# First mixer: TensorE in a written order, a head's core within the next head's projection, and key products in 32-column blocks

## The chip, the cores and the metric

The kernel runs on one core of a Trainium2 chip. The metric is device time in microseconds of one execution, the median over several runs. The engines are TensorE (PE, with its weight loads shown as PEld), VectorE (DVE), ScalarE (ACT), GpSimd (POOL) and SyncE (SP, which only issues transfers here).

## The reference

Two transformer blocks work on 256 latent and 256 context tokens of width 1024. The first block has a gated linear attention in both directions (the first mixer), the second a latent softmax attention; each is followed by a mixture of 32 experts. Only the first mixer is touched:

```python
def gla_chunkwise(q, k, v, log_f, s0):          # chunks of 32 tokens, 8 heads of 128
    def step(s, blk):
        qc, kc, vc, gc = blk
        b = jnp.cumsum(gc, axis=-2)
        b_end = b[:, :, -1:, :]
        q_dec = qc * jnp.exp(b)
        scores = jnp.einsum('bhtc,bhsc->bhts', q_dec, kc * jnp.exp(-b))
        scores = jnp.where(lower_tri, scores, 0.0)
        o = jnp.einsum('bhts,bhsv->bhtv', scores, vc) + jnp.einsum('bhtc,bhcv->bhtv', q_dec, s)
        s_new = jnp.exp(b_end[:, :, 0, :])[..., None] * s + jnp.einsum('bhsc,bhsv->bhcv', kc * jnp.exp(b_end - b), vc)
        return s_new, o
    ...

def hgrn2_mixer(h_lat, h_ctx, w_in, lower_bound, out_norm_g, w_out, with_ctx_out):
    # p = h @ w_in gives q, z_fw, z_bw, v, g; f = lb + (1 - lb) sigmoid(z); k = 1 - f
    # forward and backward passes over context and latent tokens, summed
    # y = (rms_norm(o) * silu(g)) @ w_out
    ...
```

## The kernel before

All 512 tokens stand along the free dimension, in four tiles of 128. The first mixer works through eight heads. For a head, `L507` asks for its 2 MB of weights, and four projections (`q` = forward gate, backward gate, query, output gate) are made: each is 8 contraction steps of three products (`L513` to `L515`: high part by high part, high by low, low by high), 96 products of 128x512 in all. `split` (`L262` on ACT, `L264` on DVE) makes the high and low parts of 1024 weight columns, with three buffers. The values of four heads come from a value projection of the same size (`vstep`, `L283` to `L285`), once at the start and once before head 4; it holds all four accumulators named `mm`.

`dir_pre` makes, for each direction, decayed queries `eq`, keys `ek`, keys decayed to a tile's end `ke`, and `kx`, the keys of one half of a tile decayed to the middle, for products with the other half. `core(h)` then does, for the forward direction and after it for the backward one:

- queries `qm` (`L438`, DVE) and `qt` (`L440`, `L442`);
- scores into one PSUM bank per direction (`scP`): for each tile four products with 32 columns of keys, each at its own column position of the array (`L450`), and one with a block of 64 columns (`L454`). A product of float32 operands appears in the trace as two passes;
- masking into SBUF (`L456`, DVE), and the sum over both directions (`L460`);
- turned keys (`L465`), copied by ACT (`L467`), state products (`L471`), and the running state on ACT and DVE (`L473`, `L475`). The turned keys and the state products use the single PSUM bank `p4`, one after the other.

Then come the outputs (`L487`, bank `p5`), their norm (`L492` to `L494`), and the turned output (`L498`, bank `p4`), multiplied by the gate (`L499`).

Conditioning for later stages rides along: `ada_piece` multiplies one block of `ada_w` (1 MB, `L208`) with the conditioning vector, four products at four column positions (`L212`); eight pieces make a third, which ends with a DVE sum (`L218`, for one third also `L222`) and its turned sums (`L225`). Four pieces follow each of the first six heads' projections.

The order of instructions on each engine is set by the framework's scheduler: among the instructions that are ready by its own model of time, it takes the one that stands first in the program. `tc.manual_schedule(engines=...)`, used elsewhere in the kernel, keeps the program's order on the named engines instead. So before the change, TensorE's list interleaves `core(h)` with the projection of head h + 1 as the scheduler finds them ready.

Of the kernel before, what the change touches and what calls it, by code (L numbers as in the profile page):

```python
# [9 lines left out]
F32 = mybir.dt.float32  # L10
# [6 lines left out]
ALU = mybir.AluOpType  # L17
# [65 lines left out]
class K:  # L83
# [183 lines left out]
    def hgrn(self):  # L267
        tc, nc, I = self.tc, self.nc, self.I
        PE, V, S, G = nc.tensor, nc.vector, nc.scalar, nc.gpsimd
        with ExitStack() as left, ExitStack() as st:  # L270
# [8 lines left out]
            def vstep(acc, k, H, L):  # L279
                c = slice(k % 2 * 512, k % 2 * 512 + 512)  # L280
                for tt in range(4):
                    ts = slice(tt * 128, tt * 128 + 128)
                    PE.matmul(acc[tt], hH[:, k, ts], H[:, c], start=(k == 0), stop=False)  # L283
                    PE.matmul(acc[tt], hH[:, k, ts], L[:, c], start=False, stop=False)
                    PE.matmul(acc[tt], hL[:, k, ts], H[:, c], start=False, stop=(k == 7))  # L285

            with tc.tile_pool(name="hin", bufs=1, side="right", reuse_waits="tile") as ip:
                ss = self.sp.tile([128, 4], F32, tag="ss", name="ss")
# [35 lines left out]
                for k in range(8):  # L324
                    if k % 2 == 0:
                        H, L = self.split(raw[:, k * 512:k * 512 + 1024], wp, [128, 1024])
                    vstep(acc, k, H, L)
            self.dump("hT", hH)
            cw = st.enter_context(tc.tile_pool(name="hgb", bufs=1, side="right", reuse_waits="tile"))

# [44 lines left out]
                    self.ada_piece(*ada_todo.pop(0), self.mm, aring.tile([128, 2048], F32, tag="aw", name="aw", bufs=2),  # L375
                                   lambda: [hp.tile([128, 512], F32, tag="adx", name=f"ad{t}", bufs=4) for t in "bsg"])

            def vproj(i, V4):

                acc_ = acc  # L380
                if i:
                    acc_, raw = [self.mm() for _ in range(4)], self.slot()
                    nc.sync.dma_start(raw, I["hg_wv"][i])
                    for q in range(4):
                        H, L = self.split(raw[:, q * 1024:(q + 1) * 1024], wp, [128, 1024])
                        for k in (2 * q, 2 * q + 1):
                            vstep(acc_, k, H, L)
                for tt in range(4):
                    S.copy(V4[:, tt, :], acc_[tt])

            v4 = lambda t: t.rearrange("p (t c j) -> p t c j", t=4, c=2)

            def dir_pre(h, d, z):
# [26 lines left out]
                V.tensor_tensor(ek, s, ek, op=ALU.mult)  # L420
                ex = lambda i: e[:, :, i:4:2].rearrange("p t (c o) -> p t c o", o=1)
                sq_, sk_ = (ex(0), ex(1)) if d == 0 else (ex(1), ex(0))
                ke = cw.tile([128, 512], F32, tag="ke", name="ke", bufs=2)
                V.tensor_tensor(v4(ke), v4(ek), sk_.to_broadcast([128, 4, 2, 64]), op=ALU.mult)
                first = v4(ke)[:, :, d, :]
                kx = cw.tile([128, 4, 64], F32, tag="kx", name="kx", bufs=2)
# [1 line left out]
                V.tensor_tensor(first, first, e[:, :, 5 - d:6 - d].to_broadcast([128, 4, 64]), op=ALU.mult)  # L428
                return dict(eq=eq, ek=ek, ke=ke, kx=kx, sq=sq_, E=e)

            def core(h, V4, hh, dd, sq, gs, dst):
                vs = slice(hh * 128, hh * 128 + 128)
                Sst, qts, scs = [], [], []
                both = cw.tile([128, 512], F32, tag="on", name="both")
                for d in range(2):
                    x = dd[d]
                    qm = x["eq"]
                    V.tensor_tensor(qm, sq, x["eq"], op=ALU.mult)  # L438
                    qt = cw.tile([128, 512], F32, tag="qt", name="qt", bufs=2)
                    V.tensor_tensor(v4(qt), v4(qm), x["sq"].to_broadcast([128, 4, 2, 64]), op=ALU.mult)  # L440
                    second = v4(qt)[:, :, 1 - d, :]
                    V.tensor_tensor(second, second, x["E"][:, :, 4 + d:5 + d].to_broadcast([128, 4, 64]), op=ALU.mult)  # L442
                    qts.append(qt)
                    psc = scP[d]
                    for tt in range(4):
                        a = tt * 128
                        for c in range(4):
                            s0, c0 = a + c * 32, a + (c // 2) * 64
                            t0, n = (c0, 64) if c % 2 == d else (s0, 32)
                            PE.matmul(psc[c * 32:c * 32 + 32, t0:t0 + n], x["ek"][:, s0:s0 + 32], qm[:, t0:t0 + n],  # L450
                                      start=True, stop=True, tile_position=(0, c * 32))

                        t0 = a + 64 * (1 - d)
                        PE.matmul(psc[d * 64:d * 64 + 64, t0:t0 + 64], x["kx"][:, tt, :], qm[:, t0:t0 + 64], start=True, stop=True)  # L454
                    sc = scT[d]
                    V.copy_predicated(sc.rearrange("p (t j) -> p t j", t=4), masks[d].to_broadcast([128, 4, 128]),  # L456
                                      psc.rearrange("p (t j) -> p t j", t=4))
                    scs.append(sc)
                    if d:
                        V.tensor_tensor(both, scs[0], sc, op=ALU.add)  # L460
                    order = [0, 1, 2, 3] if d == 0 else [1, 0, 3, 2]
                    pk = self.sm()
                    for i in range(3):
                        tt = order[i]
                        PE.transpose(pk[:, i * 128:(i + 1) * 128], x["ke"][:, tt * 128:(tt + 1) * 128], self.ident)  # L465
                    kT = cw.tile([128, 384], F32, tag="kT", name="kT", bufs=1)
                    S.copy(kT, pk[:, 0:384])  # L467
                    pd = self.sm()
                    for i in range(3):
                        cs = slice(i * 128, i * 128 + 128)  # L470
                        PE.matmul(pd[:, cs], kT[:, cs], V4[:, order[i], vs], start=True, stop=True)  # L471
                    ss = cw.tile([128, 3, 128], F32, tag="S", name="S", bufs=2)
                    S.copy(ss[:, 0, :], pd[:, 0:128])  # L473
                    for i in range(1, 3):
                        V.scalar_tensor_tensor(ss[:, i, :], ss[:, i - 1, :], x["E"][:, order[i], 6:7], pd[:, i * 128:(i + 1) * 128],  # L475
                                               op0=ALU.mult, op1=ALU.add)
                    Sst.append((ss, {order[i + 1]: i for i in range(3)}))
                po = self.ac()
                for tt in range(4):
                    ts = slice(tt * 128, tt * 128 + 128)  # L480
                    ops = [(both[:, ts], V4[:, tt, vs])]
                    for d in range(2):
                        ss, pos = Sst[d]
                        if tt in pos:
                            ops.append((qts[d][:, ts], ss[:, pos[tt], :]))
                    for i, (l_, r_) in enumerate(ops):
                        PE.matmul(po[:, ts], l_, r_, start=(i == 0), stop=(i == len(ops) - 1))  # L487
                ssq = cw.tile([128, 4], F32, tag="ssq", name="ssq", bufs=2)
                on = cw.tile([128, 4, 128], F32, tag="on", name="on", bufs=1)
                for tt in range(4):  # L490
                    ts = slice(tt * 128, tt * 128 + 128)
                    S.activation(on[:, tt, :], po[:, ts], AF.Square, accum_out=ssq[:, tt:tt + 1])  # L492
                ssq = self.rstd(ssq, 128, 4, "rs4")
                V.tensor_tensor(on, po.rearrange("p (t j) -> p t j", t=4),  # L494
                                ssq.rearrange("p (t o) -> p t o", o=1).to_broadcast([128, 4, 128]), op=ALU.mult)
                pt = self.sm()
                for tt in range(4):
                    PE.transpose(pt[:, tt * 128:(tt + 1) * 128], on[:, tt, :], self.ident)  # L498
                V.scalar_tensor_tensor(dst(), pt, self.cols[:, 64:65], gs, op0=ALU.mult, op1=ALU.mult)  # L499

            for h in range(8):
                if h % 4 == 0:
                    V4 = cw.tile([128, 4, 512], F32, tag="V4", name="V4", bufs=2)
                    vproj(h // 4, V4)
                dd = []
                raw = self.slot()
                nc.sync.dma_start(raw, I["hg_w"][h])  # L507
                for q in range(4):
                    H, L = self.split(raw[:, q * 1024:(q + 1) * 1024], wp, [128, 1024])
                    p = self.mm()  # L510
                    for k in range(8):
                        c = slice(k * 128, k * 128 + 128)
                        PE.matmul(p, H[:, c], hH[:, k, :], start=(k == 0), stop=False)  # L513
                        PE.matmul(p, H[:, c], hL[:, k, :], start=False, stop=False)  # L514
                        PE.matmul(p, L[:, c], hH[:, k, :], start=False, stop=(k == 7))  # L515
                    if q < 2:
                        dd.append(dir_pre(h, q, p))
                    else:
                        t = cw.tile([128, 512], F32, tag=f"sq{q}", name=f"sq{q}", bufs=2)
                        self.sigmoid(t, p, -1)  # L520
                        V.tensor_tensor(t, t, p, op=ALU.mult)
                        if q == 2:
                            sq = t
                        else:
                            gs = t
                if h < 6:
                    ada_some(4)
                o7 = []

                def dst():  # L530
                    if h < 7:
                        return oT[:, h, :]
                    o7.append(cw.tile([128, 512], F32, tag="on", name="o7"))
                    return o7[0]
                if h == 5:
                    self.load_router(hp, 0)
                if h == 7:
                    self.router(hp, 0, self.mm())
                core(h, V4, h % 4, dd, sq, gs, dst)


            wop = [self.slot() for _ in range(2)]
# [990 lines left out]
```

## Time and profile before

| | us |
|---|---|
| median of 3 runs (1575.3 to 1577.18) | 1576.33 |
| the profiled execution | 1578.04 |
| its span, first to last instruction | 1576.3 |
| TensorE busy in the span | 1499.6 |
| DVE busy in the span | 813.2 |
| ACT busy in the span | 449.1 |
| stage of the eight heads' projections | 53 to 344 |

A line of the timeline reads: start, duration, engine, line and operation, what is written and read, shapes and count, and in brackets the engine's idle time before it and what ended that. Matmuls overlap, since their ends are modelled: what a matmul costs the engine is read from the start of the next one.

### The profile page before, as it was taken

How to read it: one execution, taken by the hardware profiler on the slowest of the kernel's cores; microseconds unless marked ns; L12 is line 12 of the kernel's file. 1: busy time of each engine (PE TensorE's matmuls, PEld its weight loads, DVE VectorE, ACT ScalarE, POOL GpSimd, SP SyncE). 2: the span in 40 equal slices, each digit the busy share in tenths (PEclk: the TensorE clock that was granted, in tenths of full speed). 3: DMA queues.
4: the chain of work that ended last, by engine and by line, in shares of the span. 5: the costliest groups of instructions: out<-in, count | busy, mean ns of one | idle time of the engine just before them, and what ended most of it. 6: DMA issues, size and time to landing. Idle time of an engine off the chain costs nothing. (4 is left out here: it accounts for less than half of the span.)

```text
span 1576.3 us, 20139 instructions
## 1 busy us (share of the span) xinstructions
PE 1499.6 (95%) x8009; PEld 825.2 (52%) x8010; DVE 813.2 (52%) x1675; ACT 449.1 (28%) x938; POOL 74.9 (5%) x101
## 2 busy tenths in 40 slices
PE   7999999999899999999999999989799999998997
PEld 4777787778644544544544454447444443433433
DVE  5776647775824544544544567674534332332333
ACT  4554445553411111111111145554411111111110
POOL 0000000001300000000000011310100000000000
PEclk9999999999799999999999999999899999999999
DMA  9454534414769999999999957344799999999997
GB/s 384 165 201 177 196 136 161 188 54 161 276 240 399 429 428 426 428 427 426 427 429 423 356 218 305 141 187 142 272 392 428 427 427 428 428 427 428 427 425 268
DMA packets 63127, 500.80 MB, mean 318 GB/s; under 512 B 7024, under 2 KB 16624, under 8 KB 32816
## 3 DMA queue, kind: packets, MB, share of 16 engines
q1 hardware_dynamic: 59296, 490.87, 76.5%
q10 hardware_dynamic: 2816, 7.26, 1.4%
q0 software_dynamic: 912, 1.27, 0.3%
q8 instruction: 67, 1.10, 0.3%
q14 instruction: 36, 0.29, 0.0%
HBM read 498.26 MB, written 1.11 MB: 317 GB/s over the span
## 5 line engine op out<-in xcount | busy, mean ns | idle before, releaser
L1038 PE MATMUL mm<-w,xT 128*64 128x512 f32 x2048 | 469.9, 595 | 19.8 <-DMA w<-in_wg_dram 16.4
L1038 PEld LDWEIGHTS mm<-w,xT 128*64 128x64 f32 x2048 | 146.8, 137 | 310.7 <-issue 266.3
L1089 DVE TENSOR_TENSOR tmp<-p,rG 128x512 f32<-128x512 f32 (+1 forms) x106 | 68.0, 644 | 132.7 <-PE p L1087 132.6
L1090 DVE TENSOR_TENSOR x<-x,tmp 128x512 f32<-128x512 f32 (+1 forms) x195 | 132.4, 679 | 6.7
L1089 DVE TENSOR_TENSOR tmp<-p,x 128x512 f32<-128x512 f32 (+1 forms) x68 | 44.4, 655 | 165.1 <-PE p L1087 165.1
L1069 PE MATMUL mm<-w,x 128*64 128x512 f32 (+1 forms) x544 | 116.3, 570 | 1.6 <-ACT x L1057 1.4
L1069 PE MATMUL mm<-w,hT 128*64 128x512 f32 (+1 forms) x544 | 113.9, 570 | 1.4 <-ACT hT L1057 1.4
L889 PE MATMUL p<-sel,h2H 128*128 128x256 f32 x384 | 101.8, 300 | 1.8 <-DVE sel L879 1.8
L513 PE MATMUL mm<-hH,wH 128*128 128x512 f32 x256 | 101.9, 398 | 0.3 <-ACT wH L262 0.3
L515 PE MATMUL mm<-hH,wL 128*128 128x512 f32 x256 | 101.3, 396 | 0.5 <-DVE wL L264 0.5
L514 PE MATMUL mm<-hL,wH 128*128 128x512 f32 x256 | 100.6, 393 | 0.0
L890 PE MATMUL p<-sel,h2L 128*128 128x256 f32 x384 | 98.5, 290 | 0.0
L1076 DVE SCALAR_TENSOR_TENSOR yL<-mm,wsl,yH 128x512 fp32r<-128x512 f32 (+1 forms) x68 | 48.7, 716 | 71.6 <-ACT yH L1075 71.6
L1075 ACT ACTIVATE yH<-mm,wsl 128x512 fp32r<-128x512 f32 (+1 forms) x68 | 45.1, 663 | 123.3 <-PE mm L1069 93.2
L889 PEld LDWEIGHTS p<-sel,h2H 128*128 128x128 f32 x384 | 76.7, 200 | 5.1 <-issue 2.4
L264 DVE TENSOR_TENSOR wL<-w,wH 128x1024 fp32r<-128x1024 f32 x55 | 67.0, 1221 | 23.5 <-ACT wH L262 22.0
L1086 PE MATMUL p<-yH,G 128*128 128x512 f32 (+1 forms) x174 | 76.2, 441 | 0.9 <-DVE tmp L1089 0.9
L890 PEld LDWEIGHTS p<-sel,h2L 128*128 128x128 f32 x384 | 76.3, 199 | 1.4 <-issue 0.8
L1069 PEld LDWEIGHTS mm<-w,x 128*64 128x64 f32 x544 | 45.6, 137 | 60.0 <-issue 45.6
L262 ACT CAST wH<-w 128x1024 fp32r<-128x1024 f32 x55 | 57.3, 1047 | 63.3 <-PE mm L514 32.8
L1069 PEld LDWEIGHTS mm<-w,hT 128*64 128x64 f32 x544 | 37.5, 137 | 65.8 <-issue 59.7
L1086 PEld LDWEIGHTS p<-yH,G 128*128 128x128 f32 x174 | 32.5, 187 | 65.8 <-issue 51.5
(392 smaller groups left out, 2119.2 us busy)
## 6 DMA issues: line engine op xcount, KB each, us to landing
w<-in_wg_dram SPq DMA_DIRECT2D x52, 2048.0 KB, 18.1
w<-in_wu_dram SPq DMA_DIRECT2D x52, 2048.0 KB, 21.4
w<-in_wd_dram SPq DMA_DIRECT2D x52, 2048.0 KB, 20.2
aw<-in_ada_w_dram SPq DMA_DIRECT2D x32, 1024.0 KB, 6.0
w<-in_wd_dram SPq DMA_DIRECT2D x48, 512.0 KB, 8.7
w<-in_hg_w_dram SPq DMA_DIRECT2D x8, 2048.0 KB, 7.9
w<-in_wg_dram SPq DMA_DIRECT2D x32, 512.0 KB, 7.8
w<-in_wu_dram SPq DMA_DIRECT2D x32, 512.0 KB, 9.5
```

What stands on the lines that cost most here:

```text
L262: nc.scalar.copy(H, raw)
L264: nc.vector.tensor_tensor(L, raw, H, op=ALU.subtract)
L513: PE.matmul(p, H[:, c], hH[:, k, :], start=(k == 0), stop=False)
L514: PE.matmul(p, H[:, c], hL[:, k, :], start=False, stop=False)
L515: PE.matmul(p, L[:, c], hH[:, k, :], start=False, stop=(k == 7))
L889: self.nc.tensor.matmul(o, self.h2H[:, tt, c], r, start=(tt == 0 and k == 0), stop=False)
L890: self.nc.tensor.matmul(o, self.h2L[:, tt, c], r, start=False, stop=(last and k == 1))
L1038: PE.matmul(p[a * 64:(a + 1) * 64, :], xT[:, k, a * 64:(a + 1) * 64], ws[a][:, k * 512:(k + 1) * 512], start=(k == 0), stop=(k == 7))
L1069: PE.matmul(p[a * 64:(a + 1) * 64, :], hT[:, j, a * 64:(a + 1) * 64], ws[a][:, j * 1024 + n * w_:j * 1024 + n * w_ + w_], start=(j == 0), ...
L1086: PE.matmul(pc, g, yH, start=True, stop=False)
L1089: V.tensor_tensor(t, pc, rG[vec(tt)][:, ns], op=ALU.mult)
L1090: adder.tensor_tensor(x[:, tt, ns], x[:, tt, ns], t, op=ALU.add)
```

## The change

The loop over heads becomes generators. `project(h)` makes the four projections in 32 steps of three products, `vproj` the second half of the values in 32 steps; `core(h)` gives way seven times. `beside` runs a projection and, after fixed steps of it, the next part of the previous head's core; the conditioning pieces come two by two after steps 7 and 24. Inside this block TensorE keeps the program's order; the other engines are scheduled as before. The scores of both directions are made in one go, after both directions' `qm`. The products with `kx`, 64 columns at a time for one direction, become 32-column products: for each tile, the two halves of both directions' blocks take the four column positions. `ke` has three buffers. The last head's core runs after the block, as before.

```diff
-                ke = cw.tile([128, 512], F32, tag="ke", name="ke", bufs=2)
+                ke = cw.tile([128, 512], F32, tag="ke", name="ke", bufs=3)
...
+            def scores(dd, qms):
+                for tt in range(4):
+                    a = tt * 128
+                    for d in range(2):
+                        for c in range(4):
+                            s0, c0 = a + c * 32, a + (c // 2) * 64
+                            t0, n = (c0, 64) if c % 2 == d else (s0, 32)
+                            PE.matmul(scP[d][c * 32:c * 32 + 32, t0:t0 + n], dd[d]["ek"][:, s0:s0 + 32], qms[d][:, t0:t0 + n],
+                                      start=True, stop=True, tile_position=(0, c * 32))
+                    for c in range(4):
+                        d = c // 2
+                        t0 = a + 64 * (1 - d)
+                        PE.matmul(scP[d][c * 32:c * 32 + 32, t0:t0 + 64], dd[d]["kx"][:, tt, c % 2 * 32:c % 2 * 32 + 32],
+                                  qms[d][:, t0:t0 + 64], start=True, stop=True, tile_position=(0, c * 32))
...
-                        t0 = a + 64 * (1 - d)
-                        PE.matmul(psc[d * 64:d * 64 + 64, t0:t0 + 64], x["kx"][:, tt, :], qm[:, t0:t0 + 64], start=True, stop=True)
...
+            def beside(job, side, ada=False):
+                next(side, None)
+                for i, _ in enumerate(job, 1):
+                    if ada and i in (7, 24):
+                        ada_some(2)
+                    if i in (7, 10, 12, 14, 16, 19, 25):
+                        next(side, None)
+
+            V4, side = values(acc), iter(())
+            with tc.manual_schedule(engines={mybir.EngineType.PE}):
+                for h in range(8):
+                    if h == 4:
+                        res = []
+                        beside(vproj(res), side)
+                        V4, side = res[0], iter(())
+                    res = []
+                    beside(project(h, res), side, h < 6)
+                    side = core(h, V4, *res, dst_of(h))
+                    if h == 5:
+                        self.load_router(hp, 0)
+            self.router(hp, 0, self.mm())
+            for _ in side:
+                pass
```

In the new `core`, the places where it gives way stand: after both `qm` (before the projection starts); after scores, `qt`, masks and their sum; after the forward direction's turned keys; after its state products; after the same two of the backward direction; and after outputs and norm.

More of the change, by code (lines that the diff above doesn't have):

```diff
@@ L285, in vstep @@
                     PE.matmul(acc[tt], hL[:, k, ts], H[:, c], start=False, stop=(k == 7))
+                    yield
             with tc.tile_pool(name="hin", bufs=1, side="right", reuse_waits="tile") as ip:
@@ L326, in hgrn @@
                         H, L = self.split(raw[:, k * 512:k * 512 + 1024], wp, [128, 1024])
-                    vstep(acc, k, H, L)
+                    for _ in vstep(acc, k, H, L):
+                        pass
             self.dump("hT", hH)
@@ L376, in ada_some, with values, vproj @@
                                    lambda: [hp.tile([128, 512], F32, tag="adx", name=f"ad{t}", bufs=4) for t in "bsg"])
[L378 to L387, printed above, removed]
+            def values(acc_):
+                V4 = cw.tile([128, 4, 512], F32, tag="V4", name="V4", bufs=2)
                 for tt in range(4):
                     S.copy(V4[:, tt, :], acc_[tt])
+                return V4
+            def vproj(res):
+                acc_, raw = [self.mm() for _ in range(4)], self.slot()
+                nc.sync.dma_start(raw, I["hg_wv"][1])
+                for q in range(4):
+                    H, L = self.split(raw[:, q * 1024:(q + 1) * 1024], wp, [128, 1024])
+                    for k in (2 * q, 2 * q + 1):
+                        yield from vstep(acc_, k, H, L)
+                res.append(values(acc_))
             v4 = lambda t: t.rearrange("p (t c j) -> p t c j", t=4, c=2)
@@ L429, in dir_pre, with core @@
                 return dict(eq=eq, ek=ek, ke=ke, kx=kx, sq=sq_, E=e)
-            def core(h, V4, hh, dd, sq, gs, dst):
-                vs = slice(hh * 128, hh * 128 + 128)
-                Sst, qts, scs = [], [], []
+            def scores(dd, qms):
[12 more added lines that the diff above has]
+                                  qms[d][:, t0:t0 + 64], start=True, stop=True, tile_position=(0, c * 32))
+            def core(h, V4, dd, sq, gs, dst):
+                vs = slice(h % 4 * 128, h % 4 * 128 + 128)
+                orders = [[0, 1, 2, 3], [1, 0, 3, 2]]
+                Sst, qts, qms = [], [], []
+                for d in range(2):
+                    qm = dd[d]["eq"]
+                    V.tensor_tensor(qm, sq, qm, op=ALU.mult)
+                    qms.append(qm)
+                yield
+                scores(dd, qms)
                 both = cw.tile([128, 512], F32, tag="on", name="both")
@@ L436, in core @@
                     x = dd[d]
-                    qm = x["eq"]
-                    V.tensor_tensor(qm, sq, x["eq"], op=ALU.mult)
                     qt = cw.tile([128, 512], F32, tag="qt", name="qt", bufs=2)
-                    V.tensor_tensor(v4(qt), v4(qm), x["sq"].to_broadcast([128, 4, 2, 64]), op=ALU.mult)
+                    V.tensor_tensor(v4(qt), v4(qms[d]), x["sq"].to_broadcast([128, 4, 2, 64]), op=ALU.mult)
                     second = v4(qt)[:, :, 1 - d, :]
@@ L443, in core @@
                     qts.append(qt)
[L444 to L451, printed above, removed]
-                        t0 = a + 64 * (1 - d)
[L454 to L461, printed above, removed]
+                for d in range(2):
+                    V.copy_predicated(scT[d].rearrange("p (t j) -> p t j", t=4), masks[d].to_broadcast([128, 4, 128]),
+                                      scP[d].rearrange("p (t j) -> p t j", t=4))
+                V.tensor_tensor(both, scT[0], scT[1], op=ALU.add)
+                for d in range(2):
+                    x, order = dd[d], orders[d]
+                    yield
                     pk = self.sm()
@@ L467, in core @@
                     S.copy(kT, pk[:, 0:384])
+                    yield
                     pd = self.sm()
@@ L477, in core @@
                     Sst.append((ss, {order[i + 1]: i for i in range(3)}))
+                yield
                 po = self.ac()
@@ L495, in core @@
                                 ssq.rearrange("p (t o) -> p t o", o=1).to_broadcast([128, 4, 128]), op=ALU.mult)
+                yield
                 pt = self.sm()
@@ L499, in core, with project @@
                 V.scalar_tensor_tensor(dst(), pt, self.cols[:, 64:65], gs, op0=ALU.mult, op1=ALU.mult)
[L501 to L504, printed above, removed]
+            def project(h, res):
                 dd = []
@@ L515, in hgrn @@
                         PE.matmul(p, L[:, c], hH[:, k, :], start=False, stop=(k == 7))
+                        if k < 7:
+                            yield
                     if q < 2:
@@ L521, in hgrn, with dst_of @@
                         V.tensor_tensor(t, t, p, op=ALU.mult)
[L522 to L528, printed above, removed]
+                        res.append(t)
+                    if q == 3:
+                        res.insert(0, dd)
+                    yield
+            o7 = []
+            def dst_of(h):
                 def dst():
@@ L534, in dst @@
                     return o7[0]
[L535 to L539, printed above, removed]
+                return dst
+            def beside(job, side, ada=False):
[19 more added lines that the diff above has]
+            for _ in side:
+                pass
             wop = [self.slot() for _ in range(2)]
```

## The prediction

> **What bounds the kernel now.** I began with the page's busy shares, then took the table by stages, then the timeline of the first mixer.
>
> ```profile
> PE 1499.6 (95%) x8009; PEld 825.2 (52%) x8010; DVE 813.2 (52%) x1675; ACT 449.1 (28%) x938; POOL 74.9 (5%) x101
> ```
>
> ```profile
> 53.00:344.00 291.00, 288.89 (x1920) 216.19 (x1921) 202.76 (x374) 151.47 (x301) 5.77 (x22) 1.00 0.42 159
> 344.00:357.00 13.00, 12.11 (x121) 8.90 (x120) 9.67 (x20) 7.37 (x14) 4.15 (x4) 0.74 0.01 2
> 433.00:870.00 437.00, 433.43 (x2177) 205.24 (x2178) 202.35 (x356) 49.89 (x91) 0.00 (x0) 1.00 0.98 408
> ```
>
> The columns are the stretch, its length, busy time of PE, PEld, DVE, ACT and POOL, granted clock, DMA share and GB/s. The eight heads fill 53 to 344. There PE is idle for 2.1 of 291 us at full clock, and DMA is used for 0.42. So this stage costs what TensorE spends on it, and a microsecond less of TensorE's own time is a microsecond gained, as long as no new idle time takes its place. From 433 to 870 the expert weights keep DMA at 0.98; that stretch starts when the mixer is done and slides with it. Busy time says nothing of whether TensorE is well used, since ends are modelled and overlap, so I read starts:
>
> ```profile
> 75.92 0.64 PE L212 MATMUL mm<-aw,cS 128*32 128x512 f32 x4
> ...
> 111.38 1.92 PE L212 MATMUL mm<-aw,cS 128*32 128x512 f32 x16
> 113.12 0.29 PE L450 MATMUL p<-eq,ek 128*32 128x64 f32 x8
> 113.34 0.33 PE L454 MATMUL p<-eq,kx 128*64 128x64 f32 x2
> 113.59 0.31 PE L450 MATMUL p<-eq,ek 128*32 128x64 f32 x8
> ...
> 116.87 0.33 PE L454 MATMUL p<-eq,kx 128*64 128x64 f32 x2
> 117.13 0.50 PE L513 MATMUL mm<-hH,wH 128*128 128x512 f32 x1
> 117.46 0.40 PE L514 MATMUL mm<-hL,wH 128*128 128x512 f32 x1
> ...
> 343.23 0.39 PE L513 MATMUL mm<-hH,wH 128*128 128x512 f32 x1
> 344.14 0.39 PE L514 MATMUL mm<-hL,wH 128*128 128x512 f32 x1
> 344.68 0.49 PE L610 MATMUL mm<-rw,colBf 128*2 128x36 f32 x10
> ```
>
> A head's period is 111.38 - 75.92 = 35.46 us. A projection product starts every (344.14 - 343.23)/4 = 0.227. The first one after other work takes 117.46 - 117.13 = 0.33, and the last one before a narrow-column product 344.68 - 344.14 - 0.227 = 0.31, so a return and an entry into column mode cost about 0.1 and 0.09. The scores of a head take 117.13 - 113.12 = 4.01 us: eight rounds of 0.22 for eight 32-column passes and 0.25 to 0.26 for two passes of the 64-column block.
>
> **The scores.** Removed: per 128 tokens, two 64-column blocks (four passes). Added: four 32-column products (eight passes). A head has 96 passes after and 80 before, all in one column mode, four columns side by side.
>
> ```profile
> L450 PE MATMUL p<-eq,ek 128*32 128x64 f32 x224 | 17.4, 230 | 0.8 <-DVE eq L438 0.7
> L450 PE MATMUL p<-eq,ek 128*32 128x32 f32 x224 | 14.6, 206 | 0.0
> ```
>
> The round at 113.59 spans 0.31 from first start to last end; less one instruction's mean of 0.22 its eight starts lie within 0.09. A 512-column pass of four costs (113.12 - 111.38)/4 = 0.435, which is 0.85 ns a column, so 64 columns stream in 0.054. Where no mode change follows, the next round can start 0.09 + 0.054 = 0.145 after the first. Twelve rounds give 1.75 us a head. The lower bound is streaming alone: each column strip gets 64 + 32 + 64 columns twice, 320 x 0.85 ns = 0.27 for 128 tokens, 1.1 us a head. The upper bound keeps a round at the 0.25 of the block round: 3.0 us. I take 1.75, since it rests on the same instruction.
>
> The Trainium skill (TensorEngine Tiling, Key Properties) says that changing the tiling mode drains TensorE; the two extra 0.1s above agree. Against the change speaks the skill's TensorE: Matmul & The Clock Gate (Part 1), by which starts never come closer than about 25 ns: 96 passes would be an estimated 2.4 us a head, 5 us worse over eight heads than my sum. The starts within 0.09 for eight passes are closer than that, so the row decides here.
>
> **The written order.** Each projection has 32 steps of three products (0.68 us); the previous head's core comes after steps 7 (scores), 10 (turned keys), 12 (state products), 14 and 16 (the same for the second direction), 19 (outputs) and 25 (turned output), two conditioning pieces each after steps 7 and 24. The other blocks cost:
>
> ```profile
> 201.37 0.49 PE L465 MATMUL p<-ident,ke 128*128 128x128 f32 x3
> 201.90 0.48 ACT L467 COPY kT<-p 128x384 f32<-128x384 f32 x1 [2.01 <-PE p L465]
> 202.43 0.94 PE L471 MATMUL p<-V,kT 128*128 128x128 f32 x6
> 203.12 0.48 PE L284 MATMUL mm<-wL,hH 128*128 128x512 f32 x1
> 203.40 0.27 ACT L473 COPY S<-p 128x128 f32<-128x128 f32 x1 [1.02 <-PE p L471]
> 203.70 0.73 DVE L475 SCALAR_TENSOR_TENSOR S<-S,e,p 128x128 f32<-128x128 f32 x2 [1.98 <-ACT S L473]
> 204.58 0.52 PE L465 MATMUL p<-ident,ke 128*128 128x128 f32 x3
> 204.86 0.47 PE L284 MATMUL mm<-wL,hH 128*128 128x512 f32 x1
> ...
> 207.32 0.49 PE L487 MATMUL p<-S,qt 128*128 128x128 f32 x2
> 209.35 0.48 PE L285 MATMUL mm<-wH,hL 128*128 128x512 f32 x1
> ...
> 212.03 0.69 DVE L494 TENSOR_TENSOR on<-p,rsr 128x512 f32<-128x512 f32 x1
> 212.87 0.63 PE L498 MATMUL p<-ident,on 128*128 128x128 f32 x4
> 213.25 0.48 PE L284 MATMUL mm<-wL,hH 128*128 128x512 f32 x1
> ```
>
> A head without waits: 96 x 0.227 = 21.8; eight returns and two column entries 1.0; two conditioning blocks of 16 at 1.74, 3.5; turned keys 2 x 0.28; state products 2 x 0.69; outputs 2.03 for 18 passes, so 2.25 for 20; turned output 0.38; scores 1.75. That is 32.6, against 35.46: 2.8 us. Seven heads give 19.8, of which scores are 15.8. The eighth head runs after the projections: its scores save 2.3. There the 344 to 357 row shows a granted clock of 0.74, and
>
> ```profile
> 350.83 0.68 DVE L438 TENSOR_TENSOR eq<-sq,eq 128x512 f32<-128x512 f32 x1
> ```
>
> makes the second direction's queries, behind the first direction's DVE work; the change makes both ahead of the scores. I take 2 us for that (0 to 5). Gross gain: 24.
>
> Now the waits. TensorE no longer goes round a late operand, so what is behind it waits too, all projection products above all.
> - Turned keys, step 10 to 12: the copy at 201.90 follows, state products start 1.06 after the keys. Written distance 0.28 + 1.45 = 1.7. Nothing.
> - State products to the second direction's turned keys, which need the same single PSUM bank: 204.58 - 202.43 = 2.15 when ACT and DVE are free. Written distance 0.69 + 1.45 = 2.14. No slack, so whatever sits ahead in ACT or DVE's queue is paid. The late case is
>
> ```profile
> 128.03 0.94 PE L471 MATMUL p<-V,kT 128*128 128x128 f32 x6
> ...
> 131.47 0.52 PE L465 MATMUL p<-ident,ke 128*128 128x128 f32 x3 [0.45 <-DVE e L407]
> ```
>
> with 3.44, 1.3 more. I take 0.4 a head, 2.8 in seven (0 to 9).
> - Outputs to turned output: 212.87 - 209.35 = 3.52 at best; written 6 x 0.68 + 0.1 = 4.2, and 1.74 more with a conditioning block between. Nothing taken.
> - The last piece of a conditioning third, in projections 1, 3 and 5, is followed in the written order by its own turned sums.
>
> ```profile
> 195.20 1.06 PE L212 MATMUL mm<-aw,cS 128*32 128x512 f32 x8
> 196.33 0.69 DVE L218 TENSOR_TENSOR ads<-mm,adb 128x512 f32<-128x512 f32 x1 [4.95 <-PE mm L212]
> 198.82 0.69 DVE L222 SCALAR_TENSOR_TENSOR ads<-ads,adg 64x512 f32<-64x512 f32 x1 [1.79 <-DMA adg<-in_gffn_dram]
> 200.00 0.60 PE L225 MATMUL p<-ident,ads 128*128 128x128 f32 x4
> ```
>
> Now this is covered by projection products; then PE waits 0.1 + 0.69 + 0.1, 1.0 us twice, and 1.7 where L222 comes too: 3.7, up to 5.8 if that DMA lands as late as here behind the weight loads on SP.
> - Between heads 3 and 4 the second value projection takes four accumulators, the last of them held by head 3's gate:
>
> ```profile
> 185.12 0.68 DVE L180 TENSOR_SCALAR sq<-mm 128x512 f32<-128x512 f32 x1
> 188.72 0.68 DVE L521 TENSOR_TENSOR sq<-sq,mm 128x512 f32<-128x512 f32 x1
> ```
>
> From first read to last 4.3; three accumulators cover 2.0 of it: 2 us once (1 to 4).
> - Conditioning weights:
>
> ```profile
> aw<-in_ada_w_dram SPq DMA_DIRECT2D x32, 1024.0 KB, 6.0
> ```
>
> land in 6.0, the blocks are 15 and 17 steps apart, 10 us and more: hidden. On SP a head's own weights stand among these loads and are asked for most of a head ahead, so they have the same cover. DVE and ACT do the same operations; a third key buffer costs nothing.
>
> Sum: 24 - 2.8 - 3.7 - 2 = 15.5 us, about 16 with half of the 2.1 idle now. The profiled execution took 1578.04 (span 1576.3), 1.7 over the median; from the median of 1576.33 this gives **1560**.
>
> **Rivals.** (a) Hand-offs cost nothing and scores stream at 1.1: 24 + 5.2 less 3 gives 26, 1550; for it speaks that three of the four kinds of hand-off have slack, against it the zero slack of the other. (b) Rounds don't overlap and stay at 0.25: scores 3.0, 10 us less gain, 1570; for it speaks only that no such sequence stands in this trace. The clock-gate page's floor would be the milder form of it. (c) The bank: one PSUM bank passes between PE and ACT or DVE at the turned keys, the state products, again for the second direction, and at the turned output. If each of four hand-offs is as late as the 1.3 at 131.47, that is 5.2 a head against 2.8 gained; with the rest it ends 10 us slower, 1586. It decides at 0.8 per hand-off. DVE's 203 of 291 us speaks for some queueing; 204.58 speaks against it as the rule. (d) The gain is lost downstream, or eaten by waits just so: 1576. Against it: DMA is at 0.42 before and the expert stream waits for the mixer.
>
> **Chances.** Forecast (1553 to 1566) 0.53, (a) 0.14, (b) 0.15, (c) 0.10, (d) 0.08. Measurement tells about 0.2%, 3 us, from no change: faster 0.82, same 0.08, slower 0.10. Range 1549 to 1573, which leaves out (c), (d) and the outer part of (a).
>
> **What would show it.** Right: no 64-column form among the score rows, a head's scores in 1.5 to 2.2 us, a period of 33 to 33.5 us with conditioning, idle time of PE of 1 to 2 us in front of the turned sums, three times. Wrong: PE idle in front of turned keys or outputs above 0.8 a head, released by DVE or ACT; score rounds of 0.25; or an expert stretch that starts no earlier.

## The result, and the profile after

The changed kernel is slower: median 1592.87 us (1590.08 to 1595.62, 4 runs) against 1575.82 (1575.3 to 1577.18) beside it, a ratio of 1.0102 [1.0085, 1.0119]. 1560 was forecast, with 1573 as the upper end. The profiled execution took 1590.08 against 1578.04 before: the traces below differ by 12.0 us, since the one after is the fastest of its four runs, 2.8 below their median, and the one before lies 2.2 above 1575.82.

The page's busy shares, then the table by stages, for the changed kernel:

```profile
PE 1487.4 (94%) x8137; PEld 818.8 (52%) x8138; DVE 808.4 (51%) x1675; ACT 449.2 (28%) x938; POOL 76.1 (5%) x101
```

```profile
53.00:361.00 308.00, 275.46 (x2049) 212.44 (x2050) 202.75 (x385) 152.09 (x301) 5.78 (x22) 0.97 0.40 151
361.00:374.00 13.00, 12.08 (x153) 9.30 (x152) 10.25 (x15) 7.63 (x15) 7.03 (x6) 1.00 0.26 86
444.00:881.00 437.00, 434.01 (x2183) 205.73 (x2183) 202.29 (x356) 49.89 (x91) 0.00 (x0) 1.00 0.98 407
```

The eight heads now fill 53 to 361 instead of 53 to 344. PE is idle there for 32.5 of 308 us, where it was idle for 2.1 of 291, and the granted clock is 0.97 instead of 1.00. DVE's and ACT's busy times are nearly unchanged. The expert stretch starts 11 us later and is as long as it was: what the mixer loses is passed on. The waits of PE between 53 and 361 us name the places (total, times, longest):

```profile
PE p L483 <- DVE S L494: 11.4, 6, 1.9
PE p L225 <- DVE ads L218: 6.4, 2, 3.2
PE p L225 <- DVE ads L222: 6.2, 1, 6.2
PE p L519 <- DVE on L514: 6.4, 3, 3.2
PE mm L283 <- DVE sq L542: 1.5, 1, 1.5
```

`L483` is the turned keys, `L225` the closing transposes of a conditioning third, `L519` the turned output, `L283` the second value projection. Each of these waits ends with DVE. The scores, on the other hand, became cheaper than forecast (timeline of PE):

```profile
86.66 0.36 PE L446 MATMUL p<-eq,ek 128*32 128x64 f32 x16
86.83 0.30 PE L451 MATMUL p<-eq,kx 128*32 128x64 f32 x8
86.95 0.36 PE L446 MATMUL p<-eq,ek 128*32 128x64 f32 x16
...
87.92 0.50 PE L532 MATMUL mm<-hH,wH 128*128 128x512 f32 x1
```

The 96 passes of a head start from 86.66 on, and the next projection product starts at 87.92: 1.26 us a head, against 4.01.

One late hand-off in full (timelines of PE, ACT and DVE of the same moment):

```profile
91.85 0.83 PE L490 MATMUL p<-V,kT 128*128 128x128 f32 x6
...
93.68 0.40 PE L534 MATMUL mm<-hH,wL 128*128 128x512 f32 x1
95.98 0.52 PE L483 MATMUL p<-ident,ke 128*128 128x128 f32 x3 [1.90 <-DVE S L494]
```

```profile
91.69 0.63 ACT L183 ACTIVATE s<-s 128x512 f32<-128x512 f32 x1
92.42 0.72 ACT L405 ACTIVATE g<-s,nom 128x512 f32<-128x512 f32 x1
93.05 0.25 ACT L492 COPY S<-p 128x128 f32<-128x128 f32 x1
```

```profile
93.24 1.23 DVE L408 TENSOR_TENSOR_SCAN g<-smask,g 128x516 f32<-128x516 f32 x1 [1.56 <-ACT g L405]
94.39 0.32 DVE L494 SCALAR_TENSOR_TENSOR S<-S,e,p 128x128 f32<-128x128 f32 x1
...
95.49 0.34 DVE L494 SCALAR_TENSOR_TENSOR S<-S,e,p 128x128 f32<-128x128 f32 x1
```

The state products end at 92.68. On ACT the copy `S` stands behind the next head's sigmoid and logarithm. On DVE the two state updates stand behind the next head's scan `L408`, for which DVE itself is idle for 1.56 us, and the second update behind four more operations of the next head. They end at 95.83. The turned keys start 4.13 us after the state products, not 2.14. TensorE could have gone on with projection products; the written order doesn't let it.

The table sums the rows of each trace from the first to the last projection product ("stage"): idle time of PE, time at half clock, and the scores of the seven heads in it. "Rest" is the stage less idle time and scores, so time that the half clock adds to busy work is in it. The experiments stand in the same table.

| kernel | median us | stage | idle | half clock | scores | rest |
|---|---|---|---|---|---|---|
| before | 1575.82 | 291.2 | 1.8 | 0 | 28.1 | 261.3 |
| after | 1592.87 | 307.9 | 32.4 | 17.1 | 8.9 | 266.6 |
| e1, columns only | 1566.51 | 282.9 | 8.4 | 0 | 11.0 | 263.5 |
| e2, order only | 1600.81 | 318.2 | 32.1 | 23.9 | 16.1 | 270.0 |
| e3, no written order | 1552.72 | 273.1 | 3.5 | 0 | 8.9 | 260.7 |
| e8, e3 with 64 columns | 1562.24 | 280.4 | 3.7 | 0 | 16.1 | 260.6 |
| e4, sums later | 1578.68 | 299.1 | 23.5 | 13.7 | 8.9 | 266.7 |
| e5, steps later | 1570.53 | 286.4 | 16.9 | 6.8 | 8.9 | 260.6 |
| e6, both | 1562.39 | 278.1 | 9.5 | 0 | 8.9 | 259.7 |
| e10, positions again | 1556.54 | 272.0 | 3.5 | 0 | 8.9 | 259.6 |
| e7, own bank | 1592.24 | 310.8 | 31.4 | 23.9 | 8.9 | 270.4 |
| e9, scan behind states | 1588.30 | 307.7 | 28.6 | 27.3 | 8.9 | 270.2 |
| e11, waits filled | 1590.78 | 307.8 | 11.8 | 3.4 | 8.9 | 287.2 |

From before to after: idle +30.6, scores -19.2, rest +5.3, together +16.6 (added before rounding). After the stage 5.6 us come back (from its last product to the first expert dispatch 77.0 instead of 82.7).

### The profile page after: what moved, and what is told of

It reads as the page before. It is cut to its first block, busy times and chain, and to the rows that moved or that the text cites. A ratio compares the mean times of both kernels' runs of the same rounds, so it can differ in the third digit from the quotient of the medians.

```text
span 1588.3 us, 20379 instructions
## 1 busy us (share of the span) xinstructions
PE 1487.4 (94%) x8137; PEld 818.8 (52%) x8138; DVE 808.4 (51%) x1675; ACT 449.2 (28%) x938; POOL 76.1 (5%) x101
## 5 line engine op out<-in xcount | busy, mean ns | idle before, releaser
L1080 PEld LDWEIGHTS mm<-w,xT 128*64 128x64 f32 x2048 | 147.5, 138 | 310.8 <-issue 269.3
L532 PE MATMUL mm<-hH,wH 128*128 128x512 f32 x256 | 106.9, 418 | 0.3 <-ACT wH L262 0.3
L1128 PEld LDWEIGHTS p<-yH,G 128*128 128x128 f32 x174 | 32.5, 187 | 65.8 <-issue 51.5
```

Of the source, the lines that this page charges most:

```text
L1080: PE.matmul(p[a * 64:(a + 1) * 64, :], xT[:, k, a * 64:(a + 1) * 64], ws[a][:, k * 512:(k + 1) * 512], start=(k == 0), stop=(k == 7))
L1128: PE.matmul(pc, g, yH, start=True, stop=False)
```

## The experiments

**Which part costs, which gains.** e1: the old program text and the scheduler, with both directions' scores in one go, after both `qm` as in the change, and the 32-column blocks.

```diff
-                    psc = scP[d]
...
-                        PE.matmul(psc[d * 64:d * 64 + 64, t0:t0 + 64], x["kx"][:, tt, :], qm[:, t0:t0 + 64], start=True, stop=True)
+                scores(dd, qms)
```

> The kernel before with one part of the change: both directions' scores in one go with the key products as 32-column blocks; TensorE's order stays with the scheduler. Theory A (the written order costs, the columns gain): in the changed kernel a head's scores take 1.26 us against 4.01, so 8 x 2.75 = 22 us are saved and TensorE stays without idle time: 1554 us, 1549 to 1560. Rival B (making both directions' scores together is itself what makes VectorE late): 1570 to 1590.

Measured: 1566.51, 0.9931 [0.9914, 0.9948], between the two expectations. The scores fall by 17.1 us in the stage, but 6.6 us of new idle time stand against it. Its waits, up to 345 us and so some of them behind its stage, which ends at 336 (there the first line stands at 2.5):

```profile
PE p L440 <- DVE eq L454: 3.7, 6, 1.2
PE p L497 <- DVE both L468: 2.5, 4, 1.0
```

The scheduler starts the scores before the second direction's queries (`eq`) exist, and reaches the outputs before `both`.

e2: the changed kernel with 64-column products.

```diff
-                    for c in range(4):
-                        d = c // 2
...
+                    for d in range(2):
+                        PE.matmul(scP[d][d * 64:d * 64 + 64, t0:t0 + 64], dd[d]["kx"][:, tt, :], qms[d][:, t0:t0 + 64],
+                                  start=True, stop=True)
```

> The changed kernel with the 64-column key products put back (one per direction and tile); the written order stays. Theory A: the same idle time of about 32 us and its half-clock windows, and scores at about 4 us a head again: 1593 + 8 x 2.75 = 1615 us, 1606 to 1622. Rival B (the columns bring nothing to the time because the waits absorb them): 1588 to 1600.

Measured: 1600.81, 1.0157 [1.0138, 1.0177]: 8 us over the changed kernel, just over B's numbers and below A's, so neither holds as it stands. With both directions in one go there is one switch out of column mode a tile instead of two, so the 64-column scores take 2.29 us a head, not 4.01: theory A had left that out.

e3: the changed kernel, its TensorE order left to the scheduler.

```diff
-            with tc.manual_schedule(engines={mybir.EngineType.PE}):
+            if True:
```

> The changed kernel without the written order on TensorE; the program's text with the interleaved steps stays, so the scheduler chooses among ready instructions on all engines. Theory A: it goes round late operands, idle time in the stage of the heads falls from 32 to under 5 us: 1556 us, 1549 to 1563. Rival C (the order in which the steps stand in the program makes VectorE and ScalarE late whatever TensorE does): 1580 to 1595.

Measured: 1552.72 (1551.26 to 1557.46), 0.9844 [0.9828, 0.9861]: faster than both kernels, and 40 us below the changed one by one line. That is as theory A said, and rival C falls. The waits that are left, and the first turned keys that had waited:

```profile
PE p L483 <- DVE S L494: 1.8, 6, 0.3
PE p L519 <- DVE on L514: 1.2, 3, 0.5
```

```profile
95.31 0.52 PE L483 MATMUL p<-ident,ke 128*128 128x128 f32 x3 [0.30 <-DVE S L494]
```

VectorE's order in this stretch is nearly the same in the two kernels, and the state updates end in both some 3.4 us after the state products. The difference is that TensorE reaches the turned keys after 13 projection products instead of 6.

e8: e3 with e2's edit.

> The kernel without a written order (1552.7), its cross keys again as one 64-column product for each direction and tile. Theory A (what the columns are worth is the switches between column tiles and full width, which the traces show as 1.26 us of scores a head against 2.29 with one such switch a tile): 8 x 1.03 = 8.2 us more, 1561 (1557 to 1565). Rival E (the 32-column block is most of the gain of 24): 1569 to 1577.

Measured: 1562.24, 0.9913 [0.9883, 0.9943], as theory A said; rival E falls. So, counted from the kernel before, one round of scores a head within a program text that is interleaved with the projections gives -14, the 32 columns give another -9.5, and the written order costs +40.

**Where the written order loses.** e4: the closing transposes `L225` are called after step 30 instead of right behind their products.

```diff
+        if later is None:
+            finish()
+        else:
+            later.append(finish)
...
+                    if i == 30 and closing:
+                        closing.pop(0)()
```

> The changed kernel with one wait loosened: the turned sums that close a third of the conditioning come six steps later than its last piece (4.1 us), not right behind it. Theory A: 12.6 us of idle time in front of them and two or three half-clock windows of 3.4 us (1.7 us each) go; what stays is under 2 us: 1577 us, 1572 to 1582. Rival D (the other steps wait for the same VectorE queue, so the wait moves on to the turned outputs): 1586 to 1595.

Measured: 1578.68, 1.0013 [0.9998, 1.0028]: 14 us less, within A's range. The wait on the closing sums falls from 12.6 to 0.2; of that, 3.5 comes back at the turned output, which rises from 6.4 to 9.9 in the stage, so part of rival D is true too. The profiled executions differ by 8.3 us (1590.08 and 1581.83), and the stage by 8.8: the one is the fastest of its four runs, the other the slowest of its ten.

e5: three steps later, one number each.

```diff
-                    if i in (7, 10, 12, 14, 16, 19, 25):
+                    if i in (7, 10, 12, 17, 19, 22, 31):
```

> The changed kernel with three of the seven steps later: the second direction's turned keys at 17 in place of 14, its state products at 19 (16), the outputs at 22 (19), the turned output at 31 (25). Theory A (TensorE pays because the written places ask for results that stand behind the next head's decays in VectorE's queue): the 12.0 us of waits for the states and the 6.4 for the turned outputs go, the closing sums' 12.6 stay, and with the waits the half-clock window at 136.5 goes (1.7 us): 1592.9 - 12.0 - 6.4 - 1.7 = 1573 (1566 to 1580). Rival B (the single bank p4 and the number of hand-offs set the loss, the place of the steps does not): the waits come back at the outputs or the turned output, 1586 to 1596.

Measured: 1570.53, 0.9967 [0.9954, 0.998], as theory A said with 1573. The waits on the states and on the turned output are gone. The closing sums wait 9.8 instead of 12.6, since `ads` no longer stands behind `on`, and a new wait of 5.1 stands at the second direction's state products, for `kT`.

e6: e4 and e5 together.

> The same later steps, and the conditioning's closing transposes at step 30 of a projection instead of right behind its products. Theory A: the waits at all three places go, the half-clock windows with them, and what is left of the written order is as good as the scheduler's own: 1553 (1547 to 1562), where the kernel without a written order stands at 1552.7. Rival B: no better than the later sums alone by more than 5 us, 1572 to 1580.

Measured: 1562.39, 0.9918 [0.9894, 0.9942]: just over A's upper bound, 9 us over its 1553. The wait for `kT` stays, and the third closing sum still comes late:

```profile
PE p L500 <- ACT kT L495: 5.1, 6, 0.9
PE p L227 <- DVE ads L222: 1.8, 1, 1.8
```

The second direction's turned keys now start at 95.35, when ACT has an exponential, a weight split and the first part of a sigmoid in front of it. Their copy `kT` starts at 97.59, so it needs more than two steps.

e10: the second direction's state products, the outputs and the closing transposes are moved once more.

```diff
-                    if i in (7, 10, 12, 17, 19, 22, 31):
+                    if i in (7, 10, 12, 17, 20, 23, 31):
...
-                    if i == 30 and closing:
+                    if i == 3 and closing:
```

> The kernel with later steps and later sums (1562.4), whose profile has two waits left: 0.9 us in each of six heads for kT at the second direction's state products, 1.8 us at one closing transpose. State products at 20 instead of 19, outputs at 23 instead of 22, the closing transposes at step 3 of the next projection. Theory A (each wait is a step that comes sooner than its operand): 5.3 + 1.8 go, and nothing comes back, 1555 (1550 to 1559), level with the kernel without a written order. Rival B (a wait taken away comes back further on, at the outputs or the turned output, which are now nearer together): 1560 to 1565.

Measured: 1556.54 (1555.64 to 1557.9), 0.9873 [0.9847, 0.9898], as theory A said; rival B falls.

```profile
53.00:325.00 272.00, 268.51 (x2034) 206.49 (x2034) 199.23 (x377) 148.58 (x300) 5.75 (x22) 1.00 0.45 171
```

```profile
PE mm L290 <- DVE sq L552: 1.6, 1, 1.6
PE p L500 <- ACT kT L495: 1.0, 6, 0.2
```

PE is idle for 3.5 of 272 us again, at full clock. The written order as such costs nothing: four positions and the place of the sums cost 36 of the 40 us. It gains nothing either: its median lies 3.8 above that of e3, with overlapping intervals.

**Bank or queue.** e7: the state products write to the outputs' bank `p5`.

```diff
-                    pd = self.sm()
+                    pd = self.ac()
```

> The changed kernel with the state products in the other bank (the outputs' p5) instead of p4, steps at their old places. Theory A (VectorE's queue is what is late, the bank is only where TensorE meets it): the turned keys no longer wait, but the outputs need the second direction's last state, written at 100.08 in the first such head, and would now be reached at about 98.6: some 1.5 of each 1.9 us comes back there, 1589 (1584 to 1595). Rival B (the shared bank is the cause, as the prediction had it): the 12.0 us go and the half-clock window at 136.5 with them, 1579 (1574 to 1582).

Measured: 1592.24, 1.0099 [1.0076, 1.0123], the changed kernel's time, so another bank for the state products gains nothing. Timeline of PE and of DVE:

```profile
101.78 0.77 PE L507 MATMUL p<-V,both 128*128 128x128 f32 x2 [3.24 <-DVE S L494]
```

```profile
97.79 1.22 DVE L264 TENSOR_TENSOR wL<-w,wH 128x1024 fp32r<-128x1024 f32 x1
...
100.16 1.23 DVE L408 TENSOR_TENSOR_SCAN g<-smask,g 128x516 f32<-128x516 f32 x1 [0.22 <-ACT g L405]
101.31 0.32 DVE L494 SCALAR_TENSOR_TENSOR S<-S,e,p 128x128 f32<-128x128 f32 x1
```

The wait goes to the outputs and grows to 3.2 us a head, twice what I expected: reached earlier, the last state update now stands behind a weight split and the second scan. The product that waits, `V` by `both`, needs no state: it waits for bank `p5`, which the state products now share with the outputs. So e7 moves the shared bank and doesn't free TensorE of one; that the bank alone does not make the wait rests on e3, e5, e9 and e10, which keep `p4` and lose it.

e9: VectorE's order changes, TensorE's steps stay. (What ACT makes from the scan comes later with it.) `dir_pre` gives way ahead of its scan, which is queued behind the first direction's state updates.

```diff
+                yield
-                V.tensor_tensor_scan(gf, ...)
+                scan = V.tensor_tensor_scan(gf, ...)
+                if d == 0 and h:
+                    tc.keep_in_program_order(scan)
...
+                        if q == 1 and k == 4:
+                            next(pre, None)
```

> The changed kernel with its steps at their old places; only VectorE's order differs: the next head's scan over its first decays (1.23 us, for which VectorE stood 1.56 us idle) and all behind it stand after the two state updates of the first direction instead of ahead of them. Theory A (the queue's order is what makes the states late): S copy ends at 93.3, the two updates at about 94.0 instead of 95.83, TensorE is there at 93.9; of 1.9 us a head at most 0.4 is left, and the half-clock window behind it goes: 1592.9 - 10 - 1.7 = 1581 (1575 to 1586). Rival B (copy and two updates over one bank are too long for two steps in any order): 1.2 us or more a head stays, 1587 to 1596.

```profile
92.73 0.73 DVE L497 SCALAR_TENSOR_TENSOR S<-S,e,p 128x128 f32<-128x128 f32 x2 [1.64 <-ACT S L495]
93.38 1.23 DVE L409 TENSOR_TENSOR_SCAN g<-smask,g 128x516 f32<-128x516 f32 x1
...
109.23 0.69 DVE L218 TENSOR_TENSOR ads<-mm,adb 128x512 f32<-128x512 f32 x1
```

```profile
93.61 0.52 PE L486 MATMUL p<-ident,ke 128*128 128x128 f32 x3
...
109.97 1.12 PE L225 MATMUL p<-ident,ads 128*128 128x128 f32 x4 [4.16 <-DVE ads L218]
```

Measured: 1588.30, 1.0074 [1.0048, 1.0099]. The mechanism is as theory A said: the wait at the turned keys falls from 1.9 to 0.1 us. The time is rival B's, though not for B's reason. At the first closing sums PE is there 2.3 us earlier (at 105.81), `ads` starts only 1.35 earlier, and the third closing sum waits 8.9 us, until the load `adg` lands (DVE stands idle for it at the end). So `L225` grows from 12.6 to 17.2, the turned output with a small product just before it from 6.4 to 8.7, and half-clock time from 17.1 to 27.3. Of the 11.4 us repaired here, 4.6 are left in the time: the rest went to the next early steps and to the clock.

**The clock in the waits.** Table by stretches of the changed kernel (the figure behind the five engines is the granted clock). Half clock, 0.50, is granted from 112.6 to 116.1, 136.5 to 139.9, 187.7 to 194.6 and 286.7 to 290.1. Waits of 3.2 us end shortly before the first and the last, at 111.3 and 285.9; the one of 6.2 ends at 190.2. Of two waits of 1.9, one ends at 135.4 and has half clock behind it, the other ends at 171.8 and has not:

```profile
133.12:136.53 3.41, 1.51 (x9) 0.99 (x8) 2.36 (x8) 1.69 (x4) 0.10 (x1) 1.00 1.01 370
136.50:139.90 3.40, 3.40 (x13) 2.93 (x12) 2.61 (x6) 1.88 (x4) 0.00 (x0) 0.50 0.67 275
167.25:170.66 3.41, 2.70 (x15) 1.98 (x13) 1.85 (x5) 1.79 (x4) 0.00 (x0) 1.00 1.02 341
170.66:174.07 3.41, 2.23 (x14) 2.00 (x15) 2.32 (x7) 2.36 (x5) 0.10 (x1) 1.00 0.96 413
171.80:175.20 3.40, 3.36 (x20) 2.96 (x21) 2.42 (x5) 2.89 (x6) 0.00 (x0) 1.00 0.71 301
```

e11 keeps PE busy in the waits.

```diff
+            def fill(n):
+                for _ in range(n):
+                    PE.matmul(scP[0], hH[:, 0, 0:128], hH[:, 0, :], start=True, stop=True)
...
+                    if d and h < 7:
+                        fill(8)
...
+        if fill is not None:
+            fill(28 if g == 2 else 14)
```

> The changed kernel with needless full-width products (0.23 us each, into a bank that nobody reads by then) placed where TensorE waits: eight ahead of the second direction's turned keys, fourteen ahead of the closing transposes of two conditioning groups and twenty-eight ahead of the third. The results come no sooner, so nothing is gained from the waits themselves; TensorE is only kept busy in them. Theory A (the half-clock windows, 17.1 us of them, are set off by these idle times and cost half their length on top): the windows go, 1592.9 - 8.5 = 1584 (1580 to 1588). Rival C (the clock falls for another reason, or the windows cost nothing since TensorE waits in them anyway): 1590 to 1597.

```profile
111.00:117.00 6.00, 5.21 (x28) 4.15 (x27) 3.84 (x8) 0.00 (x0) 1.80 (x4) 1.00 0.55 219
135.00:141.00 6.00, 6.00 (x41) 5.43 (x40) 5.29 (x9) 4.25 (x8) 0.00 (x0) 1.00 0.25 107
187.00:194.00 7.00, 6.73 (x34) 5.36 (x33) 3.31 (x7) 0.00 (x0) 1.03 (x2) 1.00 0.36 138
```

Measured: 1590.78, 1.0097 [1.0077, 1.0116]; the time is rival C's. The trace tells more. The stretches at half clock went from 17.1 to 3.4 us, so the idle time had set them off. The 112 fillers take 27.9 us where the idle time fell by 20.6; the "rest" without them is 287.2 - 27.9 = 259.3, against 266.6. So these stretches had cost about 7 us (in the table the rest grows by some 10 for 24 to 27 us of half clock, so 0.4 of their length rather than the half that I took), and the fillers gave as much away again, in part since a set of eight stands beside the value projection, where nothing waits. A net gain from keeping PE busy is not shown.

## Why the prediction was wrong

- **The scores: right, and better.** 1.75 us a head was forecast with 1.1 as the lower bound; 1.26 was measured. Columns and gathering gave 19.2 us in seven heads where 15.8 was forecast. The eighth head and the tail gave 5.6 where 4.3 was forecast. The gross gain, 24.8, stood at 24, but that the totals agree is partly luck: the 24 held 4.0 us of TensorE time outside the scores, of which the runs at full clock show 0.6 to 1.7 (rest 260.7 in e3 and 259.6 in e10, against 261.3).
- **State products to turned keys: the step that failed first.** I took 0.4 us a head; it is 1.9 in six of the seven heads, 11.4 us in the stage, over the 9 given as bound. The "2.14 with ACT and DVE free" came from the row at 204.58, beside the value projection, where no next head's decays are in the queues. That is the one place that does not stand for the rule. The late case at 131.47, 3.44 us, was shown there and taken for the exception. The lateness was also put down to the single bank; e9 keeps the bank, takes the scan out of the way and loses the wait (0.1 us), so the queue makes it, and in e7 the bank decides where TensorE meets it.
- **Outputs to turned output: taken as free**, again from the quiet head ("3.52 at best"); it is 6.4 us in the stage, nearly all of it beside the last two projections (3.2 and 2.6), where no conditioning block stands in between. `on` is made behind the next head's second set of decays, at 109.38 in the profile's first such head:

```profile
108.25 1.22 DVE L264 TENSOR_TENSOR wL<-w,wH 128x1024 fp32r<-128x1024 f32 x1
109.38 0.68 DVE L514 TENSOR_TENSOR on<-p,rsr 128x512 f32<-128x512 f32 x1
109.98 0.68 DVE L542 TENSOR_TENSOR sq<-sq,mm 128x512 f32<-128x512 f32 x1
110.58 0.68 DVE L218 TENSOR_TENSOR ads<-mm,adb 128x512 f32<-128x512 f32 x1
```

- **The closing sums: 3.7 forecast, 5.8 at most; 12.6 measured.** The place and the number of waits were right, the size was not. Two of the three take 3.2 us each: the rows above show `ads` made last, at 110.58, behind the three operations over it. I had priced the operation (0.69) and two hand-overs, not its place in the queue, although the row at 196.33 was preceded by 4.95 us of idle DVE, that is by an empty queue. The third, 6.2 us, is mostly a load: `adg` is asked for at 183.6 and lands 5.0 us later, at 188.6, about as late as in the kernel before (5.5 us), which the bound had allowed for, and DVE starts `L222` 0.9 later, behind other work. With an empty queue an estimated 5.3 of the 6.2 would stay (188.6 and `L222`'s 0.7, from the products' end at 184.0).

```profile
189.46 0.68 DVE L222 SCALAR_TENSOR_TENSOR ads<-ads,adg 64x512 f32<-64x512 f32 x1
```

- **The clock: not priced.** Idle times were counted once; the half-clock windows behind them cost some 5 to 7 us more (rest +5.3 against before, about 7 by e11).
- **Right:** nothing at the first direction's turned keys; the second value projection, 1.5 where 2 was taken; conditioning weights hidden; the mixer's loss passed on to the expert stretch.
- **Rival (c)** came nearest (1586), and its own terms give more: 24 - 28 x 1.3 - 3.7 - 2 is -18, or 1594. Its place was right only in part: there is 1.9 us at one of its four hand-offs, 6.4 us in all at the turned output and nothing at the two others, and what its bank was to do the queue does. The sign of "wrong" that the prediction named, PE idle ahead of turned keys above 0.8 a head, released by DVE, is what the first line of the waits shows.

The sum with the measured terms: 24.8 gained, 30.6 lost to idle time, 5.3 to the rest: 11 slower, where the profiled executions differ by 12.0.

## What to carry to other kernels

When an engine's order is written out, each step's place has to be set by when the slowest producer really delivers in the new neighbourhood, with what will stand ahead of it in that producer's queue; a best-case hand-off read where the queue is empty is the wrong row. If the waits are there, move all the steps until the list of waits is empty: one repaired alone can hand its gain to the next (e9 kept 4.6 us of 11.4). And try the same program text without the written order first: here the gain came from the text and the columns, and the scheduler found the places by itself.

## What the hardware showed that was not expected

- Three of the changed kernel's four half-clock stretches stand behind waits of only 1.9 to 3.2 us, though there is not one behind every such wait: the waits that end at 135.4 and 171.8 are alike, and the clock behind them is 0.50 for one and 1.00 for the other. The starts 112.6, 136.5, 187.7 and 286.7 lie 23.9, 51.2 and 99.0 us apart, which is 7, 15 and 29 times 3.413. The Trainium skill (TensorE: Matmul & The Clock Gate, Part 1) tells of a free-running window of 3413 ns, and the trace agrees with that. Its rule that an idle window of about 3.4 us halves the clock is too lenient here: less idle time than that was enough. What tells the two waits apart is where they fall in these windows: counted in steps of 3.413 us from the starts, the first lies whole in the window from 133.12, which has 1.90 us of idle time, and the second is split, 0.71 and 1.18 us, over the windows from 167.25 and 170.66. (The wait of 3.2 us that ends at 322.3 is split too, 1.7 and 1.5, and has no half clock behind it.) In the stages of this case's thirteen traces, 29 such windows at full clock have 1.89 us or more of idle time on PE: behind 28 of them comes half clock (the other, in e9, has 1.92). Behind none with 1.87 or less does it come.
- In pure 32-column sequences of four column positions, 24 passes start in 0.29 us (86.66 to 86.95), 12 ns apart. The floor of about 25 ns between starts that the Trainium skill states (TensorE: Matmul & The Clock Gate, Part 1) does not hold across column positions: it would have given an estimated 2.4 us a head, and 1.26 was measured.
